# One attention output tile moved to another ring of buffers, and one input tile declared first

## The chip, the cores and the metric

The kernel runs on one core of one Trainium2 chip. The metric is the time of one execution on the device in microseconds, and the median of the executions is compared. A core has five engines with queues of their own: PE (matmul), DVE (vector), ACT (scalar, activations), POOL (GpSimd) and SP, which computes nothing and issues the DMA transfers. Each queue is worked off in order. An engine waits for another one, or for a transfer, on a semaphore. All ordinary transfers of this kernel are issued by SP.

## What is computed

One layer of a hybrid encoder on `x` (1024 tokens x 1024 features, float32): a mixer with two kinds of attention, and a gated MLP. Cut to the part around the change:

```python
o_mla = mla_attention(q, k, v)               # 8 heads, 64 values each
o_ca  = chunk_attention(cq, ck, cv, rel_bias)  # 8 heads, 64 values each
mixed = jnp.dot(jnp.concatenate([o_mla, o_ca], axis=-1), w_out[l])
x = x + g_a[:, None, :] * mixed              # residual, kept for the end
h = modulate(rmsnorm(x, g_mlp_norm[l]), sh_m, sc_m)
u = causal_dwconv(jnp.dot(h, w_up[l]), conv_w[l], conv_b[l])
gate, val = jnp.split(u, 2, axis=-1)
x = x + g_m[:, None, :] * jnp.dot(jax.nn.silu(gate) * val, w_down[l])
```

## The kernel before

Products are made of a high and a low half of each operand (`hi_of`, line 77 on ACT, and `lo_of`, line 84 on POOL or DVE), three matmuls for each pair (lines 154 to 156 in `gemm3`). The stages in order of time: conditioning and projections, attention by units (one head, 512 query tokens), the output projection with the residual, the MLP's up half in 22 steps (`ff_tile`), and the down half.

**Attention.** A unit's transposed output is summed in PSUM (`values`, line 859), scaled to a 64x512 tile `o...` by ACT (868) and DVE (869), and stored to the DRAM array `oT_d`. All units but the last store at once (873). For the last one, `om13_1`, the store is put off: `held[0]()` issues it (871) after four loads of `oT_d`. Beside the attention run fillers. The last filler is `f_oca`: for each row tile `t` it multiplies the chunk-attention half of `oT_d` with half of `w_out`, and `co{t}_{n}` (ACT, 686) goes to `part_d[t]` (store in 687).

**The turn to the output projection.** For each row tile `t` of 128 tokens: `o_load(t)` reads `oT_d[0:4]` for these tokens into `ol` (1017) and makes `oh` (77) and `ol` (84). 24 matmuls then give `op{t}` (154 to 156). DVE adds the partial product `pa{t}` (load 1110), multiplies by the gate, and adds the input tile `x1_{t}` (lines 1132, 1133, 1134). The result is stored to `x1_d` (1135), its squares are summed on ACT (1136), POOL makes the factor (119, 120), DVE scales in place (1141). Row tiles 4 to 7 read tokens 512 to 1023 of `oT_d`, and so need the put-off store. `x_load(t)` issues the loads of `pa{t}` and `x1_{t}`; tiles 0 to 3 are loaded ahead, tile `t + 4` inside the loop. Between `x_load(1)` and `x_load(2)` stands `ff_load(0)`: two loads of `w_up` (`wu`, 1086), which ACT and POOL split into `wa`, `wb`, `wd`, `wf`. After row tile 4 the pages of the MLP's input are made by transposing the normalised tiles 0 to 3 (`mod_T`, 1044 on PE, 1046 on ACT).

**Buffers.** A tile belongs to a pool and a tag, and a tag has `bufs` slots. `rtile` takes tag `R` (4 slots of 2 KB for each partition: the row tiles of the projections, last `cl7` and `ch7` of `f_oca`), `qtile` takes tag `sq` (2 slots: squares, `co` tiles, and the last unit's output). A pool opened later may lie in the memory of one that was closed; a first write then waits for the last users of the bytes underneath. The pool `tb` with the eight `x1_` slots of 4 KB lies over the attention's buffers. In the compiled program of the kernel before the slots begin at these bytes of a partition:

```
R   34624  36672  38720  40768                 cl7 34624, ch7 40768, cl6 36672, ch6 38720
sq  42816  44864                               co6_0 and co7_0 42816, co6_1 44864,
                                               om13_1 44864, co7_1 42816
x1  42496 (x1_0)  46592 (x1_7)  50688 (x1_6)  54784 (x1_5)
    58880 (x1_4)  62976 (x1_3)  67072 (x1_2)  71168 (x1_1)
A   62272 ... 70464                            raw tiles of w_out, 5 slots of 2 KB
```

So `x1_0`, 42496 to 46591, lies over the last 320 bytes of `R` and over nearly all of both `sq` slots.

**Order.** The framework does not keep the order of the program. A planner with a cost model of its own simulates the kernel, and gives each engine, in order of priority (the program's order, with offsets for the attention), the next instruction whose predecessors are set; the result is the fixed order of each queue. `tc.issue_after(i)` keeps an instruction behind `i` on its queue.

Of the kernel before, what the change touches and what calls it, by code (L numbers as in the profile page):

```python
# [13 lines left out]
F32 = mybir.dt.float32  # L14
# [10 lines left out]
P = 128  # L25
D = 1024
# [38 lines left out]
def layer_kernel(ctx, tc, I, out):  # L65
# [72 lines left out]
    def rtile(name, shape=(P, 512), dt=F32):  # L138
        return apg.tile(list(shape), dt, name=name, tag="R", bufs=4)

    def qtile(name):
        return apg.tile([P, 512], F32, name=name, tag="sq", bufs=2)
# [591 lines left out]
    class Unit:  # L734
# [101 lines left out]
        def values(u, i):  # L836

            if i % 4 == 1:
                u.pv = ps.tile([P, 512], F32, name=f"pv{u.nm}_{u.g}", tag="pv", bufs=1)
            c0 = (i % 4 - 1) * P  # L840
            todo = []
            for x in range(2):
                if (i - 1, x) not in u.pt:
                    continue
                tt, where = u.pt[i - 1, x]
                for j, at_ in where.items():
                    for h in range(2):
                        if len(at_) == 2:
                            b0, b1 = at_[0][h], at_[1][h]
                            todo.append((0, j, c0, 2 * P, tt[:, b0:b1 + 1:b1 - b0, :]))  # L850
                        else:
                            todo.append((1, j, c0 + at_[0][2] * P, P, tt[:, at_[0][h], :]))
            todo.sort(key=lambda v: v[0])
            with tc.high_priority(offset=OFF_V):
                for x, (_, j, c, w, mov) in enumerate(todo):
                    dst = u.pv[:, c:c + w]
                    if w > P:
                        dst = dst.rearrange("p (a b) -> p a b", a=2)
                    last = pe.matmul(dst, u.vst(j), mov, start=(x == 0), stop=(x == len(todo) - 1),  # L859
                                     skip_group_check=True)  # L860
                trail.append(last.ins)
                if i % 4 == 3:
                    final = u is units[-1]
                    dst = qtile(f"o{u.nm}_{u.g}") if final else \
                        at.tile([P, 512], F32, name=f"o{u.nm}_{u.g}", tag="o", bufs=1)
                    r0, r1 = (slice(64, 128), slice(0, 64)) if u.odd else (slice(0, 64), slice(64, 128))
                    inv = vscale[u.vs][1]
                    act.activation(dst[r0], u.pv[r1], AF.Copy, scale=inv[r1])
                    dve.scalar_tensor_tensor(dst[r0], u.pv[r0], inv[r0], dst[r0], op0=MUL, op1=ADD)
                    if final:  # L870
                        held.append(lambda: sp.dma_start(u.dst_d[r0, u.g * 512:(u.g + 1) * 512], dst[r0]))
                    else:
                        anchor["om"] = sp.dma_start(u.dst_d[r0, u.g * 512:(u.g + 1) * 512], dst[r0]).ins
            return 56 * sum(w // P for _, _, _, w, _ in todo)
# [109 lines left out]
    for n in range(len(tiles) + DEPTH):  # L984
        if n < len(tiles):
            u, i = tiles[n]
# [4 lines left out]
        if n >= DEPTH:  # L991
            u, i = tiles[n - DEPTH]
# [19 lines left out]
    oh, ol, ox = {}, {}, {}  # L1012
# [25 lines left out]
    tb = tbp.__enter__()  # L1038
# [68 lines left out]
    def x_load(t):  # L1107
        if t > 3:
            op_[t] = gb.tile([P, D], F32, name=f"pa{t}", tag="pa", bufs=4)
        sp.dma_start(op_[t][:], part_d[t])  # L1110
        ox[t] = tb.tile([P, D], F32, name=f"x1_{t}", tag="x1", bufs=8)
        with tc.issue_after(anchor["ol"]):
            anchor["wu"] = sp.dma_start(ox[t][:], I["x"][t * P:(t + 1) * P, :]).ins

    sp.dma_start(gabc[:], ga_d[:])
    for t in range(2):
        x_load(t)
# [3 lines left out]
    for t in range(2, 4):  # L1121
        x_load(t)
    sp.dma_start(cvp[:], I["pack"][:, C_CV:])
    for t in range(NT):
        pt = ps2.tile([P, 1024], F32, name=f"op{t}", tag="op", bufs=3)
        for n in range(2):
            gemm3(pt[:, n * 512:(n + 1) * 512],
                  [(oh[t][:, k], ol[t][:, k], wo[n][k][:, 0], wo[n][k][:, 1]) for k in range(4)])
        if t + 4 < NT:
            o_load(t + 4)  # L1130
        pa, x1 = op_[t], ox[t]
        dve.tensor_tensor(pa[:], pa[:], pt[:], op=ADD)
        dve.tensor_tensor(pa[:], pa[:], gabc[:], op=MUL)
        dve.tensor_tensor(x1[:], x1[:], pa[:], op=ADD)
        sp.dma_start(x1_d[t], x1[:])
        act.activation(pa[:], x1[:], AF.Square, accum_out=ss2[:, t:t + 1])
        if t + 4 < NT:
            x_load(t + 4)
        rsqrt_mean(r2[:, t:t + 1], ss2[:, t:t + 1], D)
        xn2[t] = x1  # L1140
        dve.tensor_scalar(x1[:], x1[:], r2[:, t:t + 1], 1.0, op0=MUL, op1=MUL)
        if t == 4:
            for k in range(ND):
                v0[k] = mod_T(k, 0)
                bpage("b11" if k < 4 else "b21", k % 4, v0[k], "v" if k % 2 else "p")
# [365 lines left out]
    for t in range(4):  # L1511
        o = dl.tile([P, 512], F32, name=f"oe{t}", tag="oe", bufs=3)
# [62 lines left out]
def build(arrays):  # L1575
    nc = bacc.Bacc("TRN2", target_bir_lowering=False, num_devices=1, dynamic_dma_scratch_size=1024)
    I = {k: nc.dram_tensor(k, v.shape, mybir.dt.from_np(v.dtype), kind="ExternalInput").ap()
         for k, v in arrays.items()}
    out = nc.dram_tensor("out_0_dram", (S, D), F32, kind="ExternalOutput").ap()
    with tile.TileContext(nc, schedule_with_timeline_sim=True) as tc, ExitStack() as ctx:  # L1580
        layer_kernel(ctx, tc, I, out)
    return nc
# [8 lines left out]
```

## Time and profile before

| | us |
|---|---|
| time, median of 3 runs | 1347.25 (1345.18 to 1351.33) |
| the profiled execution | 1345.16 |
| its span, first to last instruction | 1343.3 |
| PE busy | 1217.5 (91%) |
| DVE / ACT / POOL busy | 1091.1 / 622.5 / 581.0 |
| mean granted clock of PE | 0.955 |

The profile comes from one execution; 1.9 us of its time lie outside the span. In its timeline a row has start, duration, engine, line, operation, and `out<-in` by the program's names without their numbers (`om` is any `om...` tile, `x` in the output projection the `x1_` tiles, `op` the `op{t}` sums); `[idle before <-releaser]` is how long the engine stood idle, and what ended it. `SPq` is SP's queue, whose rows are the issues of transfers and the waits ahead of them. Times are in us from the span's start.

### The profile page before, as it was taken

Reading aid. Unit: us, or ns where it says so; the run is one execution under the profiler, and the core shown is the slowest. Engines: PE = TensorE matmul, PEld = TensorE weight load, DVE = VectorE, ACT = ScalarE, POOL = GpSimd, SP = SyncE. Lnnn points to the kernel's source line nnn. Section 1 sums busy time; section 2 is a strip of 40 time slices with the busy share of each in tenths; the row PEclk is TensorE's granted clock in tenths of the full one; section 3 lists DMA queues with packets and bytes.
Section 4 is the critical chain, followed back from the end, with each engine's and each line's share of the span. In section 5 each row is a group of like instructions: output and inputs, shape, how many; then the busy total and the mean of one; then the engine's idle time right before and its main releaser. Section 6 shows DMA issues by size and latency. Waiting matters only on the chain. (4 is left out here: it accounts for less than half of the span.)

```text
span 1343.3 us, 18699 instructions
## 1 busy us (share of the span) xinstructions
PE 1217.5 (91%) x6168; PEld 998.9 (74%) x6168; DVE 1091.1 (81%) x1928; ACT 622.5 (46%) x1132; POOL 581.0 (43%) x610
## 2 busy tenths in 40 slices
PE   4899799997867698897898999999999999999998
PEld 3888577896645577675677888888888886888886
DVE  6977898865689987894799888899999997687667
ACT  4453546443565645562375444444434444433331
POOL 5464556574656753462635454544445431000000
PEclk9899798999788899998898999999999998999999
DMA  8415677954503487778901333233333326943441
GB/s 323 138 34 117 142 172 181 194 132 100 102 26 82 102 163 163 148 160 250 354 32 63 110 119 125 102 111 109 124 111 119 126 96 230 390 155 117 131 160 63
DMA packets 223690, 190.57 MB, mean 142 GB/s; under 512 B 148709, under 2 KB 166885, under 8 KB 223593
## 3 DMA queue, kind: packets, MB, share of 16 engines
q1 hardware_dynamic: 223592, 189.38, 48.8%
q8 instruction: 48, 0.79, 0.2%
q14 instruction: 50, 0.40, 0.1%
HBM read 117.24 MB, written 37.49 MB: 115 GB/s over the span
## 5 line engine op out<-in xcount | busy, mean ns | idle before, releaser
L77 ACT ACTIVATE dnP<-dnr 128x1024 fp32r<-128x1024 f32 x73 | 77.4, 1064 | 116.9 <-PE dnA_P L1404 46.4
L1376 DVE TENSOR_TENSOR dnP<-dnr,dnP 128x1024 fp32r<-128x1024 f32 x72 | 87.9, 1224 | 52.2 <-ACT dnP L77 48.1
L73 POOL TENSOR_SCALAR hlm<-Pm,rim 128x512 f16<-128x512 f32 (+3 forms) x96 | 69.1, 729 | 79.5 <-DVE rim L800 21.9
L84 POOL TENSOR_TENSOR wf<-wu,wf 128x512 fp32r<-128x512 f32 x22 | 39.3, 1788 | 116.5 <-ACT wf L77 116.5
L1244 DVE SCALAR_TENSOR_TENSOR u<-c,cvp,u 128x1023 f32<-128x1023 f32 x44 | 64.7, 1510 | 27.5 <-ACT u L1243 26.2
L73 POOL TENSOR_SCALAR hlc<-Pc,ric 128x640 f16<-128x640 f32 (+2 forms) x64 | 52.1, 817 | 59.6 <-DVE ric L800 14.8
L819 DVE SCALAR_TENSOR_TENSOR hlm<-Pm,rim,hlm 128x512 f16<-128x512 f32 (+3 forms) x96 | 67.1, 709 | 10.0 <-POOL hlm L73 9.8
L84 POOL TENSOR_TENSOR wb<-wu,wb 128x512 fp32r<-128x512 f32 x22 | 41.0, 1862 | 64.1 <-ACT wb L77 57.9
L797 ACT ACTIVATE Pc<-sc,mc 128x640 f32<-128x640 f32 (+2 forms) x64 | 42.1, 658 | 53.3 <-DVE mc L786 32.6
L1243 ACT ACTIVATE u<-c,cvp 128x1024 f32<-128x1024 f32 x44 | 52.3, 1237 | 28.6 <-DVE c L1336 19.2
L797 ACT ACTIVATE Pm<-sm,mm 128x128 f32<-128x128 f32 (+3 forms) x64 | 47.1, 736 | 39.4 <-DVE mm L790 22.8
L1245 DVE SCALAR_TENSOR_TENSOR u<-c,cvp,u 128x1022 f32<-128x1022 f32 x44 | 63.7, 1487 | 0.0
L859 PE MATMUL pvm<-PTm,vt 128*128 128x256 f16 (+1 forms) x320 | 44.6, 289 | 16.9 <-DMA PTm<-hlm 10.9
L819 DVE SCALAR_TENSOR_TENSOR hlc<-Pc,ric,hlc 128x640 f16<-128x640 f32 (+2 forms) x64 | 51.4, 806 | 9.4 <-POOL hlc L73 9.0
L155 PE MATMUL ipq<-wq_s,hT 128*128 128x256 f32 x192 | 56.0, 293 | 0.1
L154 PE MATMUL ipq<-wq_s,hT 128*128 128x256 f32 x192 | 56.1, 295 | 0.0
L156 PE MATMUL ipq<-wq_s,hT 128*128 128x256 f32 x192 | 55.4, 289 | 0.0
L859 PEld LDWEIGHTS <-vt 128*128 128x128 f16 x320 | 31.3, 107 | 31.9 <-DMA PTm<-hlm 14.3
L77 ACT ACTIVATE wc<-ws 128x512 fp32r<-128x512 f32 x21 | 13.3, 632 | 88.6 <-DVE ws L1094 88.6
L1403 PE MATMUL dnA_P<-dnP 128*128 128x512 f32 x132 | 51.3, 389 | 0.0
L1404 PE MATMUL dnA_P<-dnP 128*128 128x512 f32 x132 | 51.3, 389 | 0.0
L1402 PE MATMUL dnA_P<-dnP 128*128 128x512 f32 x132 | 51.2, 389 | 0.0
(434 smaller groups left out, 4416.2 us busy)
## 6 DMA issues: line engine op xcount, KB each, us to landing
wu<-w_up SPq DMA_DIRECT2D x44, 512.0 KB, 3.5
dnr<-g_d SPq DMA_DIRECT2D x73, 256.0 KB, 2.8
aw<-w_ada SPq DMA_DIRECT2D x48, 256.0 KB, 3.5
g_d<-u SPq DMA_DIRECT2D x22, 512.0 KB, 3.0
dnr<-w_down SPq DMA_DIRECT2D x44, 256.0 KB, 5.4
adaw<-w_ada_a SPq DMA_DIRECT2D x16, 512.0 KB, 6.0
x<-x SPq DMA_DIRECT2D x16, 512.0 KB, 9.2
g_d<-gs SPq DMA_DIRECT2D x22, 256.0 KB, 2.7
```

The costliest lines, as they stand in the source:

```text
L73: pool.tensor_scalar(o, i, s, 1.0, op0=MUL, op1=MUL)
L77: act.activation(o, i, AF.Copy)
L84: (pool if eng == "p" else dve).tensor_tensor(o, i, f32(hi), op=SUB)
L154: pe.matmul(pt, sh, mh, start=(start and i == 0), stop=False)
L155: pe.matmul(pt, sh, ml, start=False, stop=False)
L156: last = pe.matmul(pt, sl, mh, start=False, stop=(stop and i == n - 1))
L797: act.activation(pr[:, :n], sv, AF.Exp, bias=m[:], scale=-1.0, accum_out=rsum[:, 0:1])
L819: dve.scalar_tensor_tensor(hl[:, w:2 * w], pp, ri[:], hl[:, :w], op0=MUL, op1=SUB)
L859: last = pe.matmul(dst, u.vst(j), mov, start=(x == 0), stop=(x == len(todo) - 1), skip_group_check=True)
L1244: dve.scalar_tensor_tensor(u[:, 1:], c[:, :S - 1], cvp[:, cv + 1:cv + 2], u[:, 1:], op0=MUL, op1=ADD)
L1245: dve.scalar_tensor_tensor(u[:, 2:], c[:, :S - 2], cvp[:, cv:cv + 1], u[:, 2:], op0=MUL, op1=ADD)
L1376: r = f(*a, **k)
```

## The change

The last unit's output tile is taken with `rtile` instead of `qtile`. The tile `x1_7` is declared ahead of the others, before any x tile is loaded, and `x_load(7)` uses it instead of declaring one. No instruction is added or removed.

```diff
@@ values
                     final = u is units[-1]
-                    dst = qtile(f"o{u.nm}_{u.g}") if final else \
+                    dst = rtile(f"o{u.nm}_{u.g}") if final else \
                         at.tile([P, 512], F32, name=f"o{u.nm}_{u.g}", tag="o", bufs=1)
@@ x_load
         sp.dma_start(op_[t][:], part_d[t])
-        ox[t] = tb.tile([P, D], F32, name=f"x1_{t}", tag="x1", bufs=8)
+        if t not in ox:
+            ox[t] = tb.tile([P, D], F32, name=f"x1_{t}", tag="x1", bufs=8)
         with tc.issue_after(anchor["ol"]):
             anchor["wu"] = sp.dma_start(ox[t][:], I["x"][t * P:(t + 1) * P, :]).ins
@@ after x_load
+    ox[7] = tb.tile([P, D], F32, name="x1_7", tag="x1", bufs=8)
     sp.dma_start(gabc[:], ga_d[:])
```

## Prediction

> **What bounds the kernel now.** The page comes first: one core, PE busy nearly throughout, so a gain must come from a hole in PE or from a clock that is granted in full.
>
> ```profile
> span 1343.3 us, 18699 instructions
> PE 1217.5 (91%) x6168; PEld 998.9 (74%) x6168; DVE 1091.1 (81%) x1928; ACT 622.5 (46%) x1132; POOL 581.0 (43%) x610
> ```
>
> Then I read SP's waits from 600 to 680 us, the turn that the diff touches. One wait stands out, and the view of line 1113 places it: ahead of the first x load SP stands for 8.17 us, for the landing of the last unit's store.
>
> ```profile
> SPq L1113 <- DMA oT_d<-om: 8.5, 1, 8.5
> L1113 SPq EVENT_SEMAPHORE  x1: 8172/8172/8172, 623.7 to 623.7; - x1
> ```
>
> SP's timeline shows what is queued behind it, and the view of line 871 how long the store takes to land. It is issued at 622.94 behind four `pa` loads and a `co` store, and lands 8.9 us later, at 631.8; only then do the x loads, the w_up loads and `ol4` go out, in this order.
>
> ```profile
> 619.18 2.06 SPq L1110 DMA_DIRECT2D pa<-part_d  x4
> 622.06 0.32 SPq L687 DMA_DIRECT2D part_d<-co  x1
> 622.94 0.45 SPq L871 DMA_DIRECT2D oT_d<-om  x1
> 631.93 0.81 SPq L1113 DMA_DIRECT2D x<-x  x2
> 632.79 0.90 SPq L1086 DMA_DIRECT2D wu<-w_up  x2
> 633.73 1.09 SPq L1113 DMA_DIRECT2D x<-x  x2
> 634.87 0.44 SPq L1123 DMA_DIRECT2D cvp<-pack  x1
> 635.40 0.40 SPq L1017 DMA_DIRECT2D ol<-oT_d  x1
> DMA to landing us min/median/max: 8.9/8.9/8.9
> ```
>
> Does PE pay for it? PE's timeline: `op3` ends with the matmul of 643.05, and then come two holes before row tile 4.
>
> ```profile
> 642.83 0.39 PE L155 MATMUL op<-wo,oh 128*128 128x512 f32 x1
> 643.05 0.39 PE L156 MATMUL op<-wo,ol 128*128 128x512 f32 x1
> 644.65 0.50 PE L154 MATMUL op<-wo,oh 128*128 128x512 f32 x1 [1.21 <-ACT oh L77]
> 650.33 0.79 PE L156 MATMUL op<-wo,ol 128*128 128x512 f32 x1 [4.94 <-POOL ol L84]
> 657.42 0.38 PE L1044 MATMUL ht_ps<-ident,x 128*128 128x128 f32 x2
> ```
>
> Matmuls follow each other in 0.227 us (642.83 to 643.05 before rounding), so `op4` could have started at 643.28, and its 24 matmuls would have ended at 648.7. They end at 657.42. The turn loses **8.7 us**: 6.15 in the two holes, the rest in matmuls at half clock, as the stretches show:
>
> ```profile
> 620.00:630.00 10.00, 8.89 (x38) 7.07 (x39) 3.45 (x4) 3.61 (x6) 5.06 (x4) 0.98 0.98 350
> 647.80:654.60 6.80, 4.27 (x10) 3.40 (x11) 5.41 (x5) 2.28 (x4) 6.38 (x8) 0.50 1.04 405
> ```
>
> (Columns: PE, PEld, DVE, ACT, POOL busy, granted clock, DMA share, GB/s.) The larger hole ends with POOL's low half of `ol4`. POOL and the engines before it, in their timelines:
>
> ```profile
> 619.55 0.69 DVE L84 TENSOR_TENSOR wo<-wor,wo 128x512 fp32r<-128x512 f32 x1 [5.54 <-ACT wo L77]
> 627.22 1.22 DVE L1132 TENSOR_TENSOR pa<-pa,op 128x1024 f32<-128x1024 f32 x1 [5.29 <-PE op L156]
> 628.47 1.23 DVE L1133 TENSOR_TENSOR pa<-pa,gabc 128x1024 f32<-128x1024 f32 x1
> 635.60 1.23 DVE L1134 TENSOR_TENSOR x<-x,pa 128x1024 f32<-128x1024 f32 x1 [5.91 <-DMA x<-x]
> 636.86 1.06 ACT L1136 ACTIVATE pa<-x 128x1024 f32<-128x1024 f32 x1 [12.50 <-DVE x L1134]
> 638.11 1.16 POOL L119 TENSOR_SCALAR ss<-ss 128x1 f32<-128x1 f32 x1 [11.59 <-ACT pa L1136]
> 640.87 1.29 POOL L84 TENSOR_TENSOR wa<-wu,wa 128x512 fp32r<-128x512 f32 x1
> 649.01 1.26 POOL L84 TENSOR_TENSOR ol<-ol,oh 128x512 fp32r<-128x512 f32 x1
> 643.97 0.63 ACT L77 ACTIVATE oh<-ol 128x512 fp32r<-128x512 f32 x1 [2.31 <-DMA ol<-oT_d]
> ```
>
> POOL stands idle for 11.59 us, then works off row tile 0's factor, the four w_up halves and tile 1's factor before it reaches `ol4`. The whole row hangs on the late x and w_up loads: DVE waits 5.91 us for `x1_0`.
>
> **Edit 1, the output tile in the row tiles' ring.** In the compiled program of before, `om13_1` takes 44864, `co7_1` takes 42816, and both lie under `x1_0` (42496 to 46591). Taking `om13_1` away leaves `co7_1` there, whose store is issued only 0.88 us before, so by itself this would save at most that. But ACT and PE show why `co7_1` is late:
>
> ```profile
> 601.51 0.39 PE L156 MATMUL oc<-wo,cl 128*128 128x512 f32 x1
> 618.89 0.63 ACT L77 ACTIVATE wo<-wor 128x512 fp32r<-128x512 f32 x1 [9.35 <-DMA wor<-w_out]
> 620.46 0.68 ACT L868 ACTIVATE om<-pvm,vabm 64x512 f32<-64x512 f32 x1
> 621.16 0.60 ACT L686 ACTIVATE co<-oc 128x512 f32<-128x512 f32 x1
> ```
>
> Its sum is ready at 601.9, ACT is idle for 9.35 us, even an instruction that the program has later (618.89) goes first, and `co7_1` comes right behind `om13_1`. That is what a ring does whose slots are given in the program's order of first writes: the program writes `om13_1` first, so `co7_1` waited for it. With `om13_1` in `R`, `co7_1` can follow its matmuls some 19 us earlier, and its store lands before the turn. `R` has room: `cl6` and `ch6` are free, and the slot freed first (38720) ends at 40767, below `x1_0`. Then nothing under `x1_0` is late, and the 8.17 us go. The cost: `co7_1`'s store now falls among the last transposing transfers, for which PE waits.
>
> ```profile
> 616.53 3.38 PE L859 MATMUL pvm<-PTm,vt 128*128 128x256 f16 x16 [3.22 <-DMA PTm<-hlm]
> ```
>
> If it cuts in just there, that is 0.3 us of issue and 0.75 us for 256 KB at 350 GB/s, at most 1.1 us; if it leaves the queue ahead of the put-off store, that store goes up to 0.9 us earlier. I take nothing: the sum is ready 14 us before that wait of PE ends, and the two small amounts have opposite signs.
>
> **Edit 2, x1_7 declared first.** In the compiled program slots go by first write, not by declaration: of the query pages (declared `qh0`, `qh1`, `ql`, written `qh0`, `ql`, `qh1`) `ql` has the second slot. `x1_7` is still written last, so I expect it to keep 46592, and `x1_0` 42496. If slots do go by declaration, `x1_0` to `x1_3` move down from 71168 over raw w_out tiles, whose last reader ends at 620.24 (the DVE row at 619.55), ahead of all x loads. Either way: nothing gained or lost, and no issue added.
>
> **What follows, step by step.** The planner takes SP's instructions by priority; without the wait that is `pa0`, `x1_0`, `pa1`, `x1_1`, the put-off store (ready when DVE has written it, about 622), two `wu`, then `pa2` to `x1_3`, `cvp`, `ol4`. A 512 KB load takes 1.5 us at 350 GB/s. `pa0` is there at 627.2, when DVE starts on it; `x1_0` 1.5 us later, at 628.7, before DVE is through line 1133 at 629.7. So line 1134 moves from 635.60 to 629.7, **5.9 us** earlier (if all four `pa` stay in front, 4.5 us more: 633.2, only 2.4 us earlier). ACT's squares and POOL's factor follow by the same 5.9 us. The `wu` loads land near 633.6 and 635.1 (`x1_0`, `pa1`, `x1_1`, the store, then they), so POOL starts on `wa` at 635.0 instead of 640.87. Its run from there to the end of `ol4` took 650.27 - 640.87 = 9.4 us, which gives 644.4. `ol4` itself must have landed by 642.5: four loads behind the second `wu` (6.0 us) and its own 0.75 make 641.9; just in time. PE asks for the low half at 643.28 + 2 x 0.227 = 643.7, so some **0.8 us** of the holes stay, and 8.7 - 0.8 = **7.9 us** go. This counts on full clock after so short a hole, since the half clock began only within the 4.94 us one.
>
> The Trainium skill (TensorE: Matmul & The Clock Gate, Part 1) says that PE falls to half rate after an idle window of about 3.4 us; the trace agrees with its 0.50 behind the hole of 4.94 us. By that rule a remainder of 0.8 us costs nothing more.
>
> **Does PE keep it?** Later DVE is full (the stretch below), but its work starts from PE's sums:
>
> ```profile
> 657.62 1.22 DVE L1132 TENSOR_TENSOR pa<-pa,op 128x1024 f32<-128x1024 f32 x1 [4.34 <-PE op L156]
> 669.27 1.22 DVE L1132 TENSOR_TENSOR pa<-pa,op 128x1024 f32<-128x1024 f32 x1 [1.95 <-PE op L156]
> ```
>
> ```profile
> 700.00:720.00 20.00, 14.85 (x61) 11.45 (x60) 19.96 (x33) 14.55 (x26) 6.32 (x2) 0.90 0.00 1
> ```
>
> The two rows show DVE idle until `op4` and `op6` are there, so an earlier PE moves what follows as a whole. What is late next is POOL's queue ahead of `ol4`, then the DMA rings. If the planner also brings the MLP's pages forward into these two idle times, up to 6.3 us more are won; I count none of it. The profiled execution (1345.16) would come to 1337.3; the median shown is 2.1 us higher, so 1347.25 - 7.9 = **1339.3**.
>
> **Rivals.** **B, the store behind the loads.** If the planner puts the put-off store behind `x1_0` to `x1_3` and both `wu`, 3.1 MB or 9 us are ahead of it, and `ol4`, which reads what it writes, waits. Against: its priority is above theirs. It would land near 640. `ol4` follows in 3.7 us if the queue is empty by then (as for `x1_0`, 631.93 to 635.60), in 8.6 us if it is as full as before (635.40 to 643.97); with 0.63 and 1.26 us for its halves PE goes on between 645.6 and 650.5, against 643.7 wanted. The one leaves 6.8 of the 8.7 us to win, the other nothing; halfway, with some half clock, 3.7: **1343.5** (1340.5 to 1347.3).
> The Trainium skill (DMA: Bandwidth & Descriptors, Queues, rings and completion order) speaks for B: each DMA engine takes its descriptors in the order of its ring, so earlier loads stand in front of a later store. The 8.9 us of the store agree.
>
> **C, nothing changes.** `co7_1` stays late for another reason than the ring. Then `x1_0` waits for its landing, at most 0.88 us ahead of `om13_1`'s, as the two were issued: **1346.8**.
>
> **D, slower: the planner's new order.** Row tiles 0 to 3 are normalised earlier, and the pages made of them have priority over `op5`. If all eight stand between `op4` and `op5` on PE, PE walks at ACT's pace:
>
> ```profile
> 677.05 0.78 ACT L1046 ACTIVATE hv<-ht_ps,modT 128x512 f32<-128x512 f32 x1
> 677.71 0.63 ACT L77 ACTIVATE b<-hv 128x512 fp32r<-128x512 f32 x1
> ```
>
> 8 x 1.41 = 11.3 us, of which 32 transposes at 0.19 (the row at 657.42) take 6.1 that PE spends anyway: 5.2 idle. ACT's squares and `oh` halves in the same queue (three of each, 5.1 us with the 0.63 and 1.06 above) make it 10.3, the half clock for one such stretch (6.8 us at 0.50) adds up to 3.4. It decides from 7.9 on; at 12 the time is **1351.4**. For: their priority. Against: in before they came after `op4` one by one, and some of that ACT time is saved later.
>
> **How the numbers follow.** A (forecast) 0.62, B 0.17, C 0.08, D 0.13. Half a percent, 6.7 us, is about what a measurement of this kernel can tell from no change; faster means below 1340.5. A's own spread, from all 8.7 us and the 6.3 us of pages (1332.2) to 2 us lost in queue order, puts three quarters of it below that, with a little of B 0.49; half of D lies above 1354, with scatter 0.08; the rest 0.43. The range 1332 to 1347.5 takes in A, B and C.
>
> **What would show it.** SP's wait at line 1113 gone, `co` of line 686 near 602 to 610, `x<-x` issues from about 620, line 1134 near 630, the hole at `op4` under 1.5 us with clock 1.00 at 648 to 655. Wrong if SP still waits there, if `ol4`'s hole stays over 3 us, or if a new PE hole stands between 650 and 720 us.

## The result and the profile after

| | us |
|---|---|
| before, median of 20 runs | 1347.55 (1345.06 to 1354.66) |
| after, median of 20 runs | 1343.92 (1338.3 to 1348.59) |
| ratio | 0.9966, 95% interval [0.9953, 0.9979] |
| the profiled execution after | 1345.32, span 1343.5, mean granted clock 0.948 |

By the ratio the change wins 4.6 us (2.8 to 6.3 by the interval; the two medians differ by 3.6), where 7.9 were forecast. Selected rows of SP's queue in the profile after (line 1113 is line 1114 here, and the lines from 1115 on stand 2 lower; the edits of the experiments move the numbers in the same way):

```profile
607.62 0.66 SPq L687 DMA_DIRECT2D part_d<-co  x1
620.46 1.08 SPq L667 DMA_DIRECT2D wor<-w_out  x2
621.63 2.02 SPq L1017 DMA_DIRECT2D ol<-oT_d  x4
625.19 1.33 SPq L1110 DMA_DIRECT2D pa<-part_d  x3
627.09 0.46 SPq L871 DMA_DIRECT2D oT_d<-om  x1
627.59 0.58 SPq L1110 DMA_DIRECT2D pa<-part_d  x1
628.22 0.91 SPq L1114 DMA_DIRECT2D x<-x  x2
629.90 1.62 SPq L1086 DMA_DIRECT2D wu<-w_up  x2
636.58 0.38 SPq L1017 DMA_DIRECT2D ol<-oT_d  x1
```

The wait of 8.17 us ahead of the first x load is gone, since `co7_1` is stored at 607.62. It took the place on SP of a load of `w_out`, which has moved behind the last transposing transfers, where two now stand in one row (620.46). Before, one of the two went out 13.5 us ahead of the last attention matmuls (616.53), and only one stood behind the transfers:

```profile
603.03 0.57 SPq L667 DMA_DIRECT2D wor<-w_out  x1
615.81 0.59 SPq L667 DMA_DIRECT2D wor<-w_out  x1
```

PE's timeline after shows what each side of that is worth:

```profile
621.17 3.35 PE L859 MATMUL pvm<-PTm,vt 128*128 128x256 f16 x16 [3.37 <-DMA PTm<-hlm]
626.96 0.50 PE L154 MATMUL op<-wo,oh 128*128 128x512 f32 x1 [2.44 <-ACT oh L77]
651.85 0.50 PE L156 MATMUL op<-wo,ol 128*128 128x512 f32 x1 [0.54 <-POOL ol L84]
704.51 0.50 PE L1076 MATMUL c_g<-b,wb 128*128 128x512 f32 x1 [1.65 <-DVE b L84]
```

The last 16 attention matmuls start at 616.53 us before and 621.17 after. Call this start **T**. Over the 13 profiles of this study T lies anywhere from 616.5 to 625.2 us, and from 616.5 to 624.7 even in the nine whose SP queue ahead of it is that of before; so from one profile each it can't be told whether the change gains or loses something ahead of T. The turn is therefore measured between two fixed instructions, from T to the matmul of line 1076 behind the hole of 1.65 us (after in the fence above, before in the next; the expectations below call it the first with wb, which is not exact).

```profile
704.45 0.50 PE L1076 MATMUL c_g<-b,wb 128*128 128x512 f32 x1 [1.65 <-DVE b L84]
```

The turn lasts 704.45 - 616.53 = 87.92 us before and 704.51 - 621.17 = 83.34 after, 4.58 less, close to the 4.6 of the ratio. It splits into three: `op0` starts 5.79 instead of 3.96 us after T (1.83 lost); from there to the first low product of `op4` it takes 24.89 instead of 29.84 (4.95 won); the rest 52.66 instead of 54.12 (1.46 won: no half clock behind `op4`).

DVE and POOL after, the rows that answer to those of before:

```profile
635.48 1.22 DVE L1134 TENSOR_TENSOR pa<-pa,op 128x1024 f32<-128x1024 f32 x1 [8.43 <-PE op L156]
636.74 1.22 DVE L1135 TENSOR_TENSOR pa<-pa,gabc 128x1024 f32<-128x1024 f32 x1
638.00 1.23 DVE L1136 TENSOR_TENSOR x<-x,pa 128x1024 f32<-128x1024 f32 x1
641.72 1.95 DVE L1135 TENSOR_TENSOR pa<-pa,gabc 128x1024 f32<-128x1024 f32 x1
643.71 2.20 DVE L1136 TENSOR_TENSOR x<-x,pa 128x1024 f32<-128x1024 f32 x1
645.83 1.21 DVE L1134 TENSOR_TENSOR pa<-pa,op 128x1024 f32<-128x1024 f32 x1
```

```profile
640.50 0.19 POOL L119 TENSOR_SCALAR ss<-ss 128x1 f32<-128x1 f32 x1 [8.51 <-ACT pa L1138]
641.30 1.30 POOL L84 TENSOR_TENSOR wa<-wu,wa 128x512 fp32r<-128x512 f32 x1
642.54 2.28 POOL L84 TENSOR_TENSOR wb<-wu,wb 128x512 fp32r<-128x512 f32 x1
649.53 2.27 POOL L84 TENSOR_TENSOR ol<-ol,oh 128x512 fp32r<-128x512 f32 x1
```

The first x tile's add starts 16.83 us after T (638.00), before 19.07: only **2.24 us earlier**, though its load was issued at 7.05 instead of 15.40 us after T. POOL's run from the first factor to `ol4` took 9.03 us instead of 10.90 (638.11 to 649.01 before).

Why do 8 us less of waiting move the add by 2? In the changed kernel DVE doesn't wait for the x tile: it waits 8.43 us for PE's sum `op0`, which comes 14.31 us after T instead of 10.69, and its three rows follow each other. So the late `op0` sets this add. But the tile would not have been there much earlier either, as the kernel with both tiles in R shows below (16.21, with DVE waiting for the tile). The reason is in the columns of the stretches (the last three are the granted clock, the DMA share and GB/s); first before, then after:

```profile
624.00:628.00 4.00, 4.00 (x19) 3.32 (x18) 0.78 (x1) 0.37 (x1) 2.52 (x3) 1.00 1.02 390
628.00:632.00 4.00, 4.00 (x20) 3.30 (x19) 1.66 (x2) 0.00 (x0) 0.00 (x0) 1.00 0.46 179
632.00:636.00 4.00, 4.00 (x19) 3.33 (x18) 0.40 (x1) 0.00 (x0) 0.00 (x0) 1.00 0.76 251
```

```profile
627.80:631.20 3.40, 3.40 (x9) 2.25 (x9) 0.00 (x0) 1.23 (x2) 3.40 (x4) 0.50 1.04 406
628.00:632.00 4.00, 4.00 (x12) 2.83 (x11) 0.00 (x0) 1.03 (x2) 3.99 (x4) 0.60 1.03 405
632.00:636.00 4.00, 4.00 (x20) 3.30 (x19) 0.52 (x1) 0.00 (x0) 0.00 (x0) 1.00 1.02 411
```

While SP waited, the transfer engines worked off what had been issued before. They were short of work for 0.54 x 4 + 0.24 x 4 = 3.1 us in all, and about that much can be won by issuing the same transfers earlier in the same order. `ol4` bears this out: where ACT waits for it, it comes 27.44 us after T before and 23.82 in the DVE halves of the changed kernel (below), 3.6 earlier. After, the share is 1.02 or more from 628 to 660 us.

### The profile page after: what moved, and what is told of

It reads as the page before. It is cut to its first block, busy times and chain, and to the rows that moved or that the text cites. A ratio compares the mean times of both kernels' runs of the same rounds, so it can differ in the third digit from the quotient of the medians.

```text
span 1343.5 us, 18697 instructions
## 1 busy us (share of the span) xinstructions
PE 1223.3 (91%) x6168; PEld 1002.6 (75%) x6168; DVE 1095.6 (82%) x1928; ACT 621.9 (46%) x1132; POOL 579.7 (43%) x610
## 4 chain that ended last, share of the span: by engine, by line
PE 41%; DVE 10%; issue 3%; ACT 2%; DMA 1%; POOL 1%; SPq 0%; DVEq 0%; ACTq 0%; POOLq 0%
PE p L1075 7%; PE p L1077 7%; PE p L1076 7%; PE dnA_P L1404 2%; PE dnA_P L1406 2%; PE dnA_P L1405 2%; PE dnB_P L1406 1%; PE dnB_P L1405 1%; PE dnB_P L1404 1%; DVE u L1246 1%; DVE u L1247 1%; PE dnA L1404 1%; PE op L154 1%; PE dnA L1406 1%; PE dnA L1405 1%
## 5 line engine op out<-in xcount | busy, mean ns | idle before, releaser
L797 ACT ACTIVATE Pc<-sc,mc 128x640 f32<-128x640 f32 (+2 forms) x64 | 42.1, 658 | 53.5 <-DVE mc L786 30.6
```

The lines of the kernel that those rows point to most:

```text
L797: act.activation(pr[:, :n], sv, AF.Exp, bias=m[:], scale=-1.0, accum_out=rsum[:, 0:1])
```

## Experiments

All numbers of the table but the ratios come from one profile of each kernel, in us, the first two counted from T. The changed kernel and the first edit alone are the same compiled program; their turns are 83.34 and 83.08. A ratio's scatter is as large as many of the differences, so the rows of the turn are needed beside it. But one thing in them is not the edits' doing alone: PE's clock at `op0`. Before and in the store held, PE has its full clock from the start of `op0`; in the other eleven profiles half clock lies behind it for 3.3 to 5.7 us, and it differs even between the two profiles of the same program. Here is before, then DVE halves before, each at its `op0` (the 0.94 is from the half microsecond ahead of it):

```profile
620.00:624.00 4.00, 2.89 (x11) 2.09 (x12) 1.00 (x2) 3.24 (x6) 2.54 (x3) 0.94 1.01 318
626.40:629.90 3.50, 3.36 (x7) 2.26 (x8) 0.76 (x1) 2.96 (x5) 2.94 (x3) 0.50 1.08 368
```

Half of such a stretch is lost, so PE comes to `op4` an estimated 1.7 to 2.9 us later by that alone. A hole or a turn of a single profile can be off by as much.

| kernel | first x add | `ol4` on POOL | hole at op4 to op7 | turn | ratio |
|---|---|---|---|---|---|
| before | 19.07 | 32.48 | 4.94 | 87.92 | |
| changed | 16.83 | 28.36 | 0.54 | 83.34 | 0.9966 [0.9953, 0.9979] |
| first edit alone | 16.54 | 28.08 | 0.55 | 83.08 | 0.9964 [0.9952, 0.9977] |
| both tiles in R | 16.21 | 29.53 | 1.51 | 83.04 | 0.9981 [0.9962, 1.0000] |
| x6, x7 elsewhere | 17.71 | 31.18 | 3.19 | 86.29 | 0.9982 [0.9962, 1.0001] |
| store held | 16.60 | 32.21 | 6.08 | 88.28 | 1.0003 [0.9989, 1.0017] |
| POOL order, before | 18.86 | 27.78 | 3.75 (op6) | 88.21 | 0.9986 [0.9971, 1.0000] |
| POOL order, changed | 16.96 | 25.25 | 1.48 (op6) | 84.42 | 0.9965 [0.9947, 0.9984] |
| all orders | 15.12 | 24.81 | 2.66 (op6) | 85.95 | 0.9970 [0.9953, 0.9987] |
| all orders, w_up late | 15.20 | 23.94 | 1.53 (op6) | 84.82 | 0.9951 [0.9931, 0.9971] |
| DVE halves, before | 19.14 | 28.28 | 0.88 | 82.03 | 0.9937 [0.9914, 0.9960] |
| DVE halves, changed | 16.48 | 24.53 | none | 82.17 | 0.9935 [0.9912, 0.9957] |
| DVE halves, both in R | 14.91 | 27.96 | 0.57 | 81.81 | 0.9935 [0.9912, 0.9958] |

The first theory was that of the prediction, mended by the loss at `op0`: the wait was worth some 8 us, and the `w_out` load behind the transposes takes 2 to 4 of them back. Four kernels on that.

**First edit alone.**

```diff
-                    dst = qtile(f"o{u.nm}_{u.g}") if final else \
+                    dst = rtile(f"o{u.nm}_{u.g}") if final else \
```

> Edit 1 alone; edit 2 is left out. Theory (slots go by first write, so edit 2 does nothing): the same queues as the changed kernel, SP without the 8 us wait ahead of the first x load, and the same time, ratio to before 0.995 to 0.998. Rival (edit 2 is what frees x1_0): the wait stays and the ratio is 1.000.

0.9964, as the theory had it. From 590 to 730 us its SP, ACT, DVE and POOL run the same instructions in the same order as in the changed kernel, so the second edit does nothing on top of the first. No run has the second edit alone.

**Both tiles in R.** On top of the first edit, `co7_1` goes into R. SP's order is that of before, and `op0` starts early (4.08 us after T), but `x1_0` lies over nothing late.

```diff
-                o = qtile(f"co{t}_{n}")
+                o = (rtile if (t, n) == (NT - 1, 1) else qtile)(f"co{t}_{n}")
```

> Edit 1, and the tile co7_1 in the row tiles' ring as well. Theory (in the changed kernel the early store of co7_1 takes the place of a w_out load on SP, that load goes behind the transposes, and op0 starts some 2.4 us later, with a half-clock step of some 1.7 us): here co7_1 is late as in before, the w_out load keeps its place, nothing late lies under x1_0, so op0 starts 4.0 us after the first of the last values' matmuls (5.8 in the changed kernel, 4.0 in before), the hole at op4 is under 2 us, and the ratio to before is 0.993 to 0.995, 3 to 5 us below the changed kernel. Rival (the late op0 has nothing to do with that store): op0 is late again, ratio 0.996 to 0.998.

0.9981, not the expected 0.993 to 0.995, though `op0` starts early as the theory wanted. The turn is as long as in the changed kernel although PE starts 1.7 us earlier. More half clock behind `op0` (0.50 at 628 to 632) leaves PE 0.8 us ahead at `op4`, and there it waits 1.51 us. DVE shows why:

```profile
640.18 1.22 DVE L1134 TENSOR_TENSOR x<-x,pa 128x1024 f32<-128x1024 f32 x1 [1.13 <-DMA x<-x]
```

`x1_0` was issued at 630.27 without a wait and is there at 640.18, after 9.9 us. Before it took 3.7 (631.93 to 635.60). The wait has moved from SP's queue to the transfers'.

**x6 and x7 elsewhere.** The buffers of before, but the two x tiles loaded last have slots of their own at the bottom of the pool, so `x1_0` lies higher. The other x tiles, and the later tiles that share their tag, have 6 slots instead of 8 (not shown).

```diff
+    late = {t: tb.tile([P, D], F32, name=f"x1_{t}", tag="xl", bufs=2) for t in (7, 6)}
```

> Before, with the output tile where it was; x1_6 and x1_7 get a tag of their own at the bottom of the pool, over the two square slots, and the other x tiles lie above. Theory (what counts is only which x tile lies over the late tiles): no 8 us wait ahead of x1_0, queues otherwise as in before, same time as e3_both_in_R, ratio 0.993 to 0.995. Rival (the gain needs the output tile in the other ring): ratio 1.000.

0.9982, again not the expected 0.993 to 0.995. SP's wait is gone, the add comes 1.36 us earlier, POOL's run from the first factor to `ol4` is as long as before (642.39 to 653.35, 10.96 us), and the turn is 1.6 shorter.

**Store held.** The first edit, with `co7_1`'s store put behind `ol3`, so that `w_out` is loaded in its old place.

```diff
+                if (t, n) == (NT - 1, 1):
+                    held_co.append(st_co)
...
+        held_co[0]()
```

> Edit 1, and the store of co7_1 is issued behind the four ol loads; its ACT instruction stays early. Theory (the store's place on SP costs the changed kernel its op0 start): w_out load back in its place, op0 starts some 4 us after the first of the last values' matmuls, ratio 0.993 to 0.996, the pa loads 0.7 us later than in e3_both_in_R. Rival (the early ACT instruction or the ring is the cause): op0 late as in the changed kernel, ratio 0.996 to 0.998.

1.0003: nothing is won, against every form of the first theory. SP's wait is gone, the add comes 2.47 us earlier, `op0` starts early, and the turn is 0.36 us longer than before. POOL shows where it went:

```profile
641.23 1.16 POOL L119 TENSOR_SCALAR ss<-ss 128x1 f32<-128x1 f32 x1 [9.25 <-ACT pa L1141]
642.47 1.54 POOL L120 TENSOR_TENSOR r<-ss,nhalf 128x1 f32<-128x1 f32 x1
645.24 2.27 POOL L84 TENSOR_TENSOR wb<-wu,wb 128x512 fp32r<-128x512 f32 x1
654.33 1.27 POOL L84 TENSOR_TENSOR ol<-ol,oh 128x512 fp32r<-128x512 f32 x1
```

Its run from the first factor to `ol4` takes 13.10 us, against 9.03 in the changed kernel and 10.90 before. So a second theory: **what `op4` waits for is POOL's queue**, in which two row factors and four splits of w_up stand ahead of `ol4`; when the queue may start is set by full transfer engines; SP's wait is a part of that and no cause of its own.

**POOL order, before.** Nothing but POOL's order is changed (only the lines that do it are shown).

```diff
+            with tc.issue_after(after):     # after: the low half of ol5
+                lo_of(le, w[:, 1], src, w[:, 0])
```

> The kernel before with one order changed: POOL takes the four low halves of the first w_up tiles (wa, wb, wd, wf) behind the low half of ol5 instead of ahead of that of ol4. SP's wait of 8.17 us at the x load stays, and no buffer moves. POOL theory (what holds op4 up is POOL's queue: two row factors and four splits of 1.3 to 2.3 us ahead of ol4, 10.9 us from the first factor to ol4): ol4's low half starts about 1 us after ol4 has landed (643.97 in the profile of before, where it started at 649.01), the two holes at op4, 1.21 and 4.94 us, shrink to 3 us or less in all, the half clock behind them goes, and the stretch from the last 16 matmuls of the attention to the first matmul with wb, 87.9 us before, becomes 81 to 84 us; time 0.994 to 0.997 of before. Wait theory (SP's wait, which makes x and w_up late, is what costs): the wait is still there, so the stretch stays within 1.5 us of 87.9 and the time at 0.999 to 1.001.

0.9986, turn 88.21: by these numbers the wait theory wins. The rows say otherwise. The hole at `op4` is gone, as the POOL theory has it, and comes back two tiles later; here POOL, then PE:

```profile
656.99 2.27 POOL L84 TENSOR_TENSOR wa<-wu,wa 128x512 fp32r<-128x512 f32 x1
663.15 1.29 POOL L84 TENSOR_TENSOR wf<-wu,wf 128x512 fp32r<-128x512 f32 x1
667.17 1.42 POOL L84 TENSOR_TENSOR ol<-ol,oh 128x512 fp32r<-128x512 f32 x1
```

```profile
668.64 0.80 PE L156 MATMUL op<-wo,ol 128*128 128x512 f32 x1 [3.75 <-POOL ol L84]
```

The four splits now stand ahead of `ol6`, and POOL works without a break from 655.74 to the end of that row. Here another order only moved the hole.

**POOL order, changed kernel**, the same on top of the first edit.

> The first edit (the last unit's output in R) and the same order on POOL as in the run before this one. POOL theory: in the changed kernel the hole at op4 is only 0.54 us, since there PE comes to op4 late; the stretch goes from 83.3 us to 82 to 83.3 us, time 0.995 to 0.997 of before, so the edit adds nothing, or at most 1 us, to what the order on POOL gives alone. Wait theory: the edit and the order on POOL are worth something each, and the two together 0.990 to 0.994.

0.9965, as the changed kernel. The turn of 84.42 is 1.1 us above the expected 82 to 83.3, by the same hole at `op6` (1.48 us).

**All orders**: both tiles in R, POOL's order, and `pa2`, `pa3` behind the first x and w_up loads; and **all orders, w_up late**, where w_up is loaded behind `x1_4`.

```diff
+        if 2 <= t < 4:
+            with tc.issue_after(anchor["wu"]):
+                sp.dma_start(op_[t][:], part_d[t])
```

> Both the last unit's output and co7_1 in R, the order on POOL as in the two runs above, and the loads of pa2 and pa3 (512 KB each) moved on SP behind those of x1_0, x1_1 and the two of w_up. Transfer theory (the 16 DMA engines are full from 624 us on, share 1.01 and more, so a tile lands when the bytes ahead of it are through): with 1 MB less ahead of it the first x tile's add starts at 13.5 to 14.8 us after the last 16 attention matmuls instead of 16.2 with the same buffers; ol4 has landed when PE comes to op4, no hole above 1.5 us there, and the stretch is 79 to 81.5 us (83.0 with the same buffers and the old orders); time 0.991 to 0.994 of before. If the moment of issue decides instead, the add starts at 15.5 us or later, and the stretch is above 82 us.

> As the run above, and the two loads of w_up (512 KB each), with their splits, moved behind the load of x1_4. Transfer theory: another 1 MB less ahead of ol4, which lands 2 us or more earlier than there; PE comes to op4 at about 27 us after the last 16 attention matmuls and finds it ready, so the gain over the run above is small, 0 to 1.5 us: stretch 78.5 to 80.5 us, time 0.990 to 0.993 of before. It is worse than the run above only if the splits of w_up, now later, hold up the first matmuls with wa (at 675 to 680 us), which would show as a hole there of more than 1.5 us.

0.9970 and 0.9951. Both turns missed what was expected by over 4 us, for the hole at `op6`. The add, at 15.12 and 15.20, no longer waits for the x tile but for PE's sum, so this bounds the landing from above only. The time of the second is better than its turn explains (3.1 us of 6.6); why is open.

So the last three take the work off POOL.

**DVE halves, before**: the kernel before, its wait and its buffers, with the four low halves made by DVE.

```diff
+        le = "p" if j else "v"
-        return raw, split(raw[0][:, :512], f"wa{j}", tag), split(raw[0][:, 512:], f"wb{j}", tag)
+        return raw, split(raw[0][:, :512], f"wa{j}", tag, le), split(raw[0][:, 512:], f"wb{j}", tag, le)
...
+    w21 = split(raw0[1][:, :512], "wd_0", le="v")
+    w22 = split(raw0[1][:, 512:], "wf0", le="v")
```

> The kernel before with the four low halves of the first w_up tiles (wa, wb, wd, wf) made by DVE instead of POOL; SP's wait of 8.17 us and all buffers stay. POOL theory (POOL has more work than time between op4 and op7, since its splits take 1.3 us alone and up to 2.3 us beside DVE's row work; putting them behind ol5 only carried the hole from op4 to op6): with 5 to 9 us less on POOL no low half of ol4 to ol7 is late, the holes at op4 shrink to 2.5 us or less and none comes at op5 to op7, no half clock; DVE pays 4 x 0.69 us and gets back about 1 us for each collision that goes. The stretch from the last 16 attention matmuls to the first matmul with wb, 87.9 us before and 88.2 with the splits behind ol5, becomes 81 to 84 us; time 0.993 to 0.997 of before. Wait theory: x is as late as before, so the stretch stays at 86.5 or more and the time at 0.998 to 1.001. If DVE is as full as POOL, the hole comes back at op5 to op7 behind DVE's row work, or at line 1044 or 1076, and the stretch is 85 to 88.

**0.9937, turn 82.03**, 5.9 us less than before, with the wait still there. The view of SP's x line, then DVE, POOL and PE:

```profile
L1114 SPq EVENT_SEMAPHORE  x1: 8816/8816/8816, 629.0 to 629.0; - x1
```

```profile
641.47 1.23 DVE L1135 TENSOR_TENSOR x<-x,pa 128x1024 f32<-128x1024 f32 x1 [4.78 <-DMA x<-x]
646.74 0.68 DVE L84 TENSOR_TENSOR wb<-wu,wb 128x512 fp32r<-128x512 f32 x1
```

```profile
643.97 1.16 POOL L119 TENSOR_SCALAR ss<-ss 128x1 f32<-128x1 f32 x1 [11.98 <-ACT pa L1137]
650.61 1.53 POOL L84 TENSOR_TENSOR ol<-ol,oh 128x512 fp32r<-128x512 f32 x1 [1.29 <-ACT oh L77]
```

```profile
652.20 0.50 PE L156 MATMUL op<-wo,ol 128*128 128x512 f32 x1 [0.88 <-POOL ol L84]
```

SP stands 8.82 us, DVE waits 4.78 us for `x1_0`, and the add comes 19.14 us after T, as late as before. Still the hole is 0.88 us: POOL is idle when `ol4`'s high half arrives. This separates the theories: most of the loss is gone although SP's wait is still there. What is left of the wait is this hole, since ACT now waits for the landing of `ol4`, issued behind SP's wait. PE comes late to it here, by the half clock at `op0`; at full clock the hole would be some 2.6 us (an estimate, 0.88 and half of the 3.5 us). So the wait is not shown to be free. Nor does the run tell POOL's shorter queue from the collisions with DVE that go with it (last section).

**DVE halves, changed kernel**, the same on the first edit.

> The first edit and the four low halves on DVE. POOL theory: op4's hole of 0.54 us goes and no other comes; PE then runs through from op0, whose late start (5.8 us after the last 16 attention matmuls) stays: stretch 82 to 83.3 us, time 0.994 to 0.9965 of before, within 1.5 us of the run above, so that most of what the edit gains is gained by taking work off POOL without it. Wait theory: the edit's gain stands beside whatever this gives, and this kernel is 3 us or more ahead of the run above.

0.9935, turn 82.17: the edit adds nothing measurable to what this gives alone. The hole at `op4` is gone, and `op0` starts 1.6 us later.

**DVE halves, both in R**, with `pa2` and `pa3` late.

> Both tiles in R (op0 starts about 4.3 us after the last 16 attention matmuls, and SP doesn't wait), the four low halves on DVE, and the loads of pa2 and pa3 behind those of the first two x tiles and of w_up. If PE alone bounds the stretch once buffers, POOL and the order of loads are out of the way, there is no hole above 1 us at op4 to op7 and no half clock behind op0, and the stretch is 79 to 81.5 us; time 0.990 to 0.994 of before, better than every kernel so far. If DVE has become the bound, the holes come back between 655 and 690 us at op6, op7, line 1044 or 1076, and the stretch is 82 us or more.

0.9935, turn 81.81: by 0.3 us outside what was expected of PE as the only bound; the hole stays under 1 us as expected, but the half clock behind `op0` is there. Its add, which waits for the x tile, comes 1.3 us earlier than with both tiles in R alone; 1 MB at 400 GB/s would be 2.6. The three last kernels can't be told apart by time. Their ratios are some 0.3% below that of the changed one, but the intervals just overlap, so a lead over it is likely and not shown.

## Why the prediction was right and wrong

The range held the time, which says little: 1332 to 1347.5 also took in the case that nothing changes (C). The gain is below the half percent set beforehand, so the time fell into the class that was given 0.43. It lies nearest to B's 1343.5, but B did not happen. By its steps:

- **Edit 1 frees `co7_1`**: right. ACT writes a `co` tile at 606.54 (profile after) and SP stores it at 607.62, as the ring argument said; SP's wait at the x load is gone.

```profile
606.54 0.60 ACT L686 ACTIVATE co<-oc 128x512 f32<-128x512 f32 x1 [1.82 <-PE oc L156]
```

- **Edit 2 does nothing**: right on top of the first edit, as the first edit alone shows; that slots go by first write is argued.
- **"I take nothing" for `co7_1`'s store among the transposes**: wrong in mechanism. What the store changed is SP's order; it took the place on SP of a `w_out` load, whose tile then came last ahead of `oh0` on ACT (idle for 10.06 us until 624.27). `op0` started 1.83 us later, 3.4 us of half clock at 627.8 to 631.2 fell into it, and its sum reached DVE 3.62 us later. That set the first add and brought PE to `op4` some 3 us late. Yet with `op0` early little would have been won: both tiles in R, where the add waits for the tile, has it at 16.21 instead of 16.83 and nearly the same turn, since PE then waits at `op4`. This is argued from that run, whose half clock differs; none isolates it.
- **Line 1134 5.9 us earlier**: the step that failed. It took `op0` to come as before and `x1_0` to need only its own 1.5 us at 350 GB/s behind `pa0`. Neither held: `op0`'s sum came 3.62 us late, and with the engines full `x1_0` took 9.9 us from issue to use (both tiles in R), as it needs the bytes issued ahead of it. All four `pa` did stay ahead of `x1_0`, and the bracket for that case (2.4 us earlier) is close to the measured 2.24; that is luck in part, since the changed kernel's add waited for `op0`.
- **The hole of 0.8 us** (0.7 by the prediction's own times, 644.4 - 643.7): 0.54, with clock 1.00 behind it, but by luck. `ol4`'s low half should have ended at 644.4, 27.9 us after T; it ended 30.6 after T (651.80). PE was to come 27.2 after T and came 30.1 after it (651.31). Both slid by some 3 us, so the hole fitted, and 4.6 us were won instead of 7.9.
- **POOL's run taken over as 9.4 us**: from the start of `wa` to the end of `ol4` it took 10.50 (641.30 to 651.80), and `wa` started 4.2 us earlier after T instead of 5.9. These two make up the slide of the low half. Here also lay the larger gain, unseen: the run was taken as a fixed length behind a late start, and the kernel with DVE halves shows that the four splits could be taken out of it.
- **Rivals**: B fell (the put-off store is issued ahead of the x loads), C fell with the wait, and D's transposes opened no hole above 0.5 us between `op4` and 675 us.

The compiled order could not be known before; the full transfer engines could: the stretch that the prediction itself quotes has a share of 0.98 at 620 to 630.

## What to carry to other kernels

Before a queue's wait is costed, read the DMA share while it stands: what can be won by issuing the same transfers earlier is about the time in which the transfer engines are short of work (3.1 us here), not the length of the wait (8.17). Then follow the hole to the engine that ends it and add up everything queued there ahead of the awaited instruction; taking work off that engine was worth 5.9 us of the turn, moving it back in the same queue only moved the hole. Where scatter is as large as the effect, measure a stage between two fixed instructions in the profiles, and read the granted clock in it before two stages are compared.

## Unexpected in the hardware

**POOL and DVE hold each other up.** In the changed kernel a split on POOL takes 1.30 us (641.30) or 2.28 (642.54), and DVE's line 1136 takes 1.23 or 2.20. Where the two run side by side at least one of them is long; line 1134, which reads PSUM, stays at 1.21 to 1.22 (rows above). On DVE the split takes 0.68. The Trainium skill (SBUF — State Buffer, SBUF: two separate sides) says that POOL and those DVE instructions that read two inputs from SBUF take a shared pair of ports as an exclusive lock, each blocking the other for a whole instruction; the rows agree.

**The same hole costs 2.7 us or nothing.** A hole of 3.5 us stands in every kernel 13 us behind the turn. Before, then DVE halves before:

```profile
717.46 0.80 PE L1075 MATMUL p<-t,wd 128*128 128x512 f32 x1 [3.50 <-ACT c L1198]
717.80:724.60 6.80, 6.80 (x20) 5.33 (x20) 6.73 (x6) 4.30 (x6) 5.57 (x3) 0.63 0.28 90
```

```profile
717.37 0.50 PE L1075 MATMUL p<-t,wd 128*128 128x512 f32 x1 [3.47 <-ACT c L1199]
717.80:724.60 6.80, 6.80 (x31) 5.52 (x30) 6.73 (x6) 4.21 (x6) 5.53 (x3) 1.00 0.28 95
```

At clock 0.63 PE gets through 20 matmuls, at 1.00 through 31. The twentieth matmul, counted from the one behind the hole, starts 6.98 us after it before and 7.16 in the changed kernel, but 4.50 in DVE halves before, in the first edit alone and in the store held: 2.5 to 2.7 us more. In the ten profiles that pay it is 1.5 to 2.8. What follows the turn took 638.85 us before (1343.3 - 704.45) and 635.74 here (1340.1 - 704.36); the first edit alone, also at full clock there, took 1342.2 - 706.87 = 635.3, and the changed kernel, the same program, 638.99. The Trainium skill (TensorE: Matmul & The Clock Gate, Part 1) says that idle time is judged in windows of about 3.4 us that run freely; a hole of just that length may or may not fill one, and that fits. So some 2.7 of the 3.7 us between the two profiles of one program come from there.
